# Mixture of experts: one rotating pool of tiles against fixed places with all weight loads on SyncE

## The chip, the cores and the metric

The kernel runs on one core of a Trainium2 chip. The metric is the device time of one execution in microseconds. TensorE is called PE, VectorE DVE, ScalarE ACT, GpSimd POOL and SyncE SP in the rows; PEld is PE's weight load. A "q" behind an engine's name (ACTq, SPq) marks its sequencer, which issues DMAs.

## The reference

One decoder layer on 1024 tokens of width 1024, all in float32. Three token mixers and a memory cross attention come first, each followed by a layer norm. The change lies in the last part, the routed experts: each token picks the best of 4 groups and the two best of the 8 experts in it, and the results of its two experts are added with their weights. The router is left out here:

```python
def one_expert(x_blk, ex):
    hidden = jax.nn.silu(x_blk @ w_gate[ex]) * (x_blk @ w_up[ex])   # 1024 -> 256
    return hidden @ w_down[ex]                                      # 256 -> 1024
# 32 experts; every token goes to 2 of them
y = jnp.einsum('nk,nkd->nd', expert_w, y_of_assignments)
x = layer_norm(alpha * x + y, ln3_g, ln3_b)
```

## The kernel before

The program is unrolled and runs in stages; the experts' stage (`moe`) follows the second layer norm with the router (`out_ln_route`) and is followed by the last layer norm (`final`). The normed rows stand in HBM twice: `x2d`, from which experts gather, and `acc`, to which experts add.

For each of the 32 experts up to 128 rows are gathered. Their steps, with the names that the planner gives them:

- `L`: the expert's weights come in six pieces of 128 x 1024 float32 (512 KB): four hold a quarter of gate and up (two DMAs of 256 KB), two hold half of down (one DMA). `moe_load` issues them.
- `SA`, `SD`: PE reads float32 in one quick pass only in a rounded format, so a piece is split into a rounded high part (ACT, line 1887) and the rest (DVE, line 1890), and three matmuls are made in place of one (lines 1645 to 1647). Experts 0 and 1 are not split but read whole (line 1643).
- `G`, `GQ`: the rows are gathered from `x2d` by an indirect DMA on POOL's queue (line 1616). `RT`, `RA`, `RD`: PE transposes them, ACT and DVE split them.
- `U` 0 to 3: the gate and up product with pieces 0 to 3. `YA`, `YD`: SiLU times up into a row tile `m_y`. `HT`, `HA`, `HD`: the hidden rows are transposed and split.
- `N` 0, 1: the down product with pieces 4 and 5. `EA`, `ED`: the result is scaled into the same `m_y`, half on ACT and half on DVE.
- `C`, `CQ`: an indirect DMA on POOL's queue adds `m_y` to `acc` (line 1706). The next scatter waits until this one has landed.

The order of all instructions on the five engines is fixed: `Plan.run` plays the tasks through with given lengths and lags and calls each task's function in the order of the start that it finds. Engine "Q" of the plan stands for the DMA engines.

Tiles of 4 KB a partition (`slot`) all come from one pool, `b4`, of 45 places. A tile gets a place when the function that needs it is called, and takes over the place of a tile that has been released; the first instruction that writes it waits for the last one that used the place. For an `m_y` that is the landing of its scatter. In the plan `SLOTS` (11) is the number of places that are to be had beside those of pieces already loaded and gathered rows; a load takes 1, a split 2, `YA` 1, and each gives back when done. 28 pieces are loaded by SP while the router still runs (`BEFORE`); the others are issued by ACT, in ACT's own order:

```python
def load(e, i):
    raw.setdefault(e, []).append(moe_load(k, ins, e, i, None, nc.scalar))

def split_hi(e, i):
    w[e, i] = [slot(k, "s" + n, (128, 2, HALF), F32R) for n in "hl"]
    nc.scalar.activation(w[e, i][0], raw[e][i], AF.Copy)
```

`overflow_blocks` is a loop for experts with more than 128 rows. The count is read at run time, and in the profiled execution its body doesn't run.

Of the kernel before, what the change touches and what calls it, by code (L numbers as in the profile page):

```python
# [8 lines left out]
F32 = mybir.dt.float32  # L9
# [1747 lines left out]
def overflow_blocks(k, ins, x2d, acc):  # L1757
    nc, tc = k.nc, k.tc
    n = nc.values_load(k.on[0:1, 0:1], min_val=0, max_val=15)
    with tc.If(n > 0), tc.For_i(0, n, 1) as i:  # L1760
        ids, firsts = overflow_list(k)
        e = nc.values_load(ids[0:1, bass.ds(i, 1)], engines=(E.SP,), min_val=0, max_val=NE - 1)
        raw, xg = slot(k, "m_raw", (128, 2, 2 * FF)), slot(k, "m_xg")
        parts = [slot(k, "m_w" + x, (128, 2, 2 * FF), F32R) for x in "hl"]

        first = k.sm.tile([128, 1], F32, tag="o_f", bufs=1)
        sel = k.sm.tile([128, 16], F32, tag="o_sel", bufs=1)
        nc.vector.tensor_scalar(sel, k.io128[:, 0:16], k.octr, None, op0=OP.is_equal)
        nc.vector.tensor_tensor(sel, sel, firsts, op=OP.mult)
        nc.vector.reduce_sum(first, sel, axis=AX.X)  # L1770
        nc.vector.tensor_scalar(k.octr, k.octr, 1.0, None, op0=OP.add)
        key = k.sm.tile([128, NT, 2], F32, tag="o_key", bufs=1)
        nc.vector.tensor_scalar(key, k.key, first, 1.0 / NE, op0=OP.subtract, op1=OP.mult)
        ps = k.ps.tile([128, 512], F32, tag="r")
        for t in range(NT):
            for j in range(2):
                nc.vector.tensor_scalar(k.R[j], k.io128, key[:, t, j:j + 1], None, op0=OP.is_equal)
                nc.tensor.matmul(ps[:, 0:2], k.R[j], k.ent[:, t, j], start=(t == 0 and j == 0),
                                 stop=(t == NT - 1 and j == 1))
        tab = k.sm.tile([128, 2, 1], F32, tag="o_tab", bufs=1)  # L1780
        slot_table(k, tab, ps[:, 0:2, None])
        nc.gpsimd.memset(xg, 0.0)
        moe_gather(k, tab, xg, x2d)

        def piece(j):
            return split_big(k, moe_load(k, ins, bass.ds(e, 1), j, raw), parts)

        for _ in moe_up(k, moe_rows(k, xg), piece, xg):
            pass
        _, h, _ = moe_hidden(k, xg)  # L1790
        _, pss = moe_down(k, h, lambda f: piece(4 + f))
        for n in range(2):
            moe_scale(k, pss, xg, tab, n)
        moe_scatter(k, xg, tab, acc)


class Plan:
# [4 lines left out]
    def __init__(self, slots, rest):  # L1802
        self.slots, self.rest, self.tasks, self.rank = slots, rest, {}, {}

    def add(self, name, engine, length, before=(), f=None, lag=0.15, take=0, give=0, release=0.0, rank=None):
        self.rank[name] = rank
        self.tasks[name] = engine, length, [b for b in before if (b[1] if b[0] == "then" else b) in self.tasks], f, lag, take, give, release

    def run(self):
        tail, after, need = {}, {n: [] for n in self.tasks}, {}  # L1810
        for n, (_, _, before, *_) in self.tasks.items():
            need[n] = len(before)
            for b in before:
                if b[0] == "then":
                    after[b[1]].append((n, 0))
                else:
                    after[b].append((n, 1))
        for n in reversed(self.tasks):
            tail[n] = self.tasks[n][1] + max((tail[m] + l * self.tasks[n][4] for m, l in after[n]), default=0.0)
            if self.rank[n] is not None:  # L1820
                tail[n] = self.rank[n]
        ready = {n: t[7] for n, t in self.tasks.items() if not need[n]}
        free, given, slots = {}, [], self.slots
        while ready:
            best = None
            for n, at in ready.items():
                e, _, _, _, _, take, _, _ = self.tasks[n]
                at = max(at, free.get(e, 0.0))
                if take:
                    have, rest = slots, self.rest if n[0] == "LS" else 0  # L1830
                    for g, m in given:
                        if have >= take + rest and g > at:
                            break
                        have += m
                        if have - m < take + rest:
                            at = max(at, g)
                    if have < take + rest:
                        continue
                first = ready[n] if e == "Q" else -tail[n]
                if best is None or (at, first) < best[:2]:  # L1840
                    best = at, first, n
# [4 lines left out]
            slots -= take  # L1846
            while given and given[0][0] <= at:
                slots += given.pop(0)[1]
            if give:
                given = sorted(given + [(at + length + lag, give)])  # L1850
# [9 lines left out]
def moe(k, ins, raw, x2d, acc):  # L1860

    nc = k.nc
    tab = [k.tabs[:, :, e:e + 1] for e in range(NE)]
    with k.tc.manual_schedule(engines=MOE_MANUAL):
# [9 lines left out]
    overflow_blocks(k, ins, x2d, acc)  # L1874

    P = Plan(SLOTS, REST)
    w, x, up, y, hid, h, down, pss = {}, {}, {}, {}, {}, {}, {}, {}

# [3 lines left out]
    def load(e, i):  # L1882
        raw.setdefault(e, []).append(moe_load(k, ins, e, i, None, nc.scalar))

    def split_hi(e, i):
        w[e, i] = [slot(k, "s" + n, (128, 2, HALF), F32R) for n in "hl"]
        nc.scalar.activation(w[e, i][0], raw[e][i], AF.Copy)  # L1887

    def split_lo(e, i):
        nc.vector.tensor_tensor(w[e, i][1], raw[e][i], w[e, i][0].bitcast(F32), op=OP.subtract)  # L1890

    def weights(e, i):
        return [raw[e][i]] if whole(e, i) else w.pop((e, i))
# [17 lines left out]
    def start_up(e):  # L1911
        up[e] = moe_up(k, x[e], lambda j: weights(e, j))
# [16 lines left out]
    order = [(e, i) for e in range(NE - LATE) for i in range(6)]  # L1929
    order += [(e, i) for p in (range(4), range(4, 6)) for e in range(NE - LATE, NE) for i in p]  # L1930
    for n, (e, i) in enumerate(order):
        if BEFORE[7][1] <= n < THEN:
            P.add(("L", e, i), "Q", 1.46, [], None, 0.9, release=FIRST)
        if n >= THEN:
            P.add(("LS", e, i), "A", 0.05, [("then", ("LS", *order[n - 1])), ("then", ("L", *order[n - AHEAD]))],
                  lambda e=e, i=i: load(e, i), 1.5, take=1, release=FIRST)
            P.add(("L", e, i), "Q", 1.46, [("LS", e, i)], None, 0.9)
    for e in range(NE):
        time = [1.72 if whole(e, i) else 1.3 for i in range(6)]
        for i in range(6):  # L1940
            if not whole(e, i):
                late = [] if e < SOON else [("U", e - 1, min(i, 3))]
                P.add(("SA", e, i), "A", 0.95, [("L", e, i)] + late, lambda e=e, i=i: split_hi(e, i), take=2)
                P.add(("SD", e, i), "D", 1.14, [("SA", e, i)], lambda e=e, i=i: split_lo(e, i), give=1)
        if e > 1:
            P.add(("G", e), "P", 1.04, [("RT", e - XG, 1)], lambda e=e: moe_gather(k, tab[e], k.xg[e % XG], x2d), 0.7,
                  release=4.0 * e if e < XG else 0.0)
            P.add(("GQ", e), "Q", 1.46, [("G", e)], None, 1.0)
        for g in range(2):
            P.add(("RT", e, g), "E", 0.44, [("GQ", e), ("RA", e - 1, g), ("RD", e - 1, g)],  # L1950
                  lambda e=e, g=g: rows(e, g), release=5.3 + 2.1 * e if e < 2 else 0.0)
            P.add(("RA", e, g), "A", 0.48, [("RT", e, g), ("U", e - 2, 3)], lambda e=e, g=g: rows_hi(e, g))
            if not whole(e, 0):
                P.add(("RD", e, g), "D", 0.6, [("RA", e, g)], lambda e=e, g=g: rows_lo(e, g))
        for j in range(4):
            before = [("L", e, j), ("SD", e, j), ("RA", e, j // 2), ("RD", e, j // 2), ("YD", e - 2), ("U", e, j - 1)]
            P.add(("U", e, j), "E", time[j], before, (lambda e=e: next(up[e])) if j else (lambda e=e: start_up(e)),
                  give=1 if whole(e, j) else 2)
        P.add(("YA", e), "A", 0.26, [("U", e, 3)], lambda e=e: silu(e), take=1)
        P.add(("YD", e), "D", 0.34, [("YA", e)], lambda e=e: next(up.pop(e)))  # L1960
        P.add(("HT", e), "E", 0.22, [("YD", e), ("HA", e - 1), ("HD", e - 1)], lambda e=e: start_hidden(e))
        P.add(("HA", e), "A", 0.26, [("HT", e), ("N", e - 1, 1)], lambda e=e: hidden_hi(e))
        if not whole(e, 4):
            P.add(("HD", e), "D", 0.34, [("HA", e)], lambda e=e: next(hid.pop(e)))
        for f in range(2):
            before = [("L", e, 4 + f), ("SD", e, 4 + f), ("HA", e), ("HD", e), ("EA", e - 1), ("ED", e - 1), ("N", e, f - 1)]
            P.add(("N", e, f), "E", time[4 + f], before, (lambda e=e: next(down.pop(e))) if f else (lambda e=e: start_down(e)),
                  give=1 if whole(e, 4 + f) else 2)
        P.add(("EA", e), "A", 0.57, [("N", e, 1)], lambda e=e: moe_scale(k, pss[e], y[e], tab[e], 0))
        P.add(("ED", e), "D", 0.66, [("N", e, 1)], lambda e=e: moe_scale(k, pss[e], y[e], tab[e], 1))  # L1970
        P.add(("C", e), "P", 1.04, [("EA", e), ("ED", e), ("CQ", e - 1)],
              lambda e=e: moe_scatter(k, y.pop(e), tab[e], acc), 0.7)
        P.add(("CQ", e), "Q", 1.46, [("C", e)], None, 1.0, give=1)
# [4 lines left out]
SLOTS, REST = 11, 1  # L1978
LATE = 2
WHOLE = (0, 1), (0, 1)  # L1980
AHEAD, FIRST, THEN = 3, 4.0, 28
XG = 4
SOON = 2
# [237 lines left out]
```

## Time and profile before

| | |
|---|---|
| time, median of 3 runs | 2030.04 us (2027.97 to 2032.48) |
| the profiled execution: time, span | 2029.34 us, 2027.6 us |
| before the experts / experts / last layer norm | 0 to 1617 / 1617 to 1991 / 1991 to 2028 us |
| PE, DVE, ACT busy over the span | 92%, 60%, 41% |
| DMA | 265.95 MB, mean 131 GB/s |

Times inside the profile are counted from the span's start. The profiled execution's time is 1.7 us more than its span: what lies before the first and behind the last instruction. A busy share over the whole span mixes stages with different limits, so the rows below are taken from the experts' stage alone.

### The profile page before, as it was taken

The numbers are of one execution on the slowest core, as the hardware profiler recorded it, in microseconds if no ns is written. First come the engines' busy times: TensorE is split into PE (matmuls) and PEld (weight loads), VectorE is DVE, ScalarE is ACT, GpSimd is POOL, SyncE is SP. The second block draws the span as 40 slices with busy tenths as digits, with TensorE's granted clock in tenths as the row PEclk, the third lists the DMA queues.
The fourth block names the chain that finished last, engine by engine and source line by source line (L and its number), as shares of the span: only waits on it lengthen the run. The fifth ranks groups of instructions, "written<-read, shape, count | busy, mean of one in ns | idle before, by whom it ended". The sixth has DMA issues, their size and how long they took to land. (4 is left out here: it accounts for less than half of the span.)

```text
span 2027.6 us, 26514 instructions
## 1 busy us (share of the span) xinstructions
PE 1874.6 (92%) x9820; PEld 1521.3 (75%) x9820; DVE 1213.4 (60%) x2629; ACT 840.3 (41%) x1454; POOL 224.1 (11%) x261
## 2 busy tenths in 40 slices
PE   7999999999999999999989999899989689998890
PEld 6777787787877788888877788888877557876670
DVE  3244376676766543424455767544577648997885
ACT  3433232333332353535443312433421148876773
POOL 2000000000000010000003100000001222332310
PEclk8999999999999999999999999999999899999995
DMA  4113123232314122122525323710345577999995
GB/s 129 33 32 84 42 83 79 63 99 63 99 53 105 57 63 73 53 84 68 167 84 200 119 101 108 197 28 25 115 166 179 188 254 248 294 308 313 303 302 187
DMA packets 201653, 265.95 MB, mean 131 GB/s; under 512 B 24490, under 2 KB 132200, under 8 KB 201520
## 3 DMA queue, kind: packets, MB, share of 16 engines
q1 hardware_dynamic: 148992, 149.45, 23.6%
q10 hardware_dynamic: 39264, 86.07, 12.3%
q0 software_dynamic: 13264, 28.71, 6.0%
q8 instruction: 78, 1.28, 0.3%
q14 instruction: 55, 0.45, 0.1%
HBM read 228.95 MB, written 51.97 MB: 139 GB/s over the span
## 5 line engine op out<-in xcount | busy, mean ns | idle before, releaser
L142 PE MATMUL ps<-thh,hi 128*128 128x512 f32 x1152 | 467.7, 406 | 5.2 <-ACT hi L52 1.9
L143 PE MATMUL ps<-thl,hi 128*128 128x512 f32 x1152 | 456.4, 396 | 0.0
L144 PE MATMUL ps<-thh,lo 128*128 128x512 f32 x1152 | 455.7, 396 | 0.0
L142 PEld LDWEIGHTS ps<-thh,hi 128*128 128x128 f32 x1152 | 218.0, 189 | 51.5 <-issue 6.0
L144 PEld LDWEIGHTS ps<-thh,lo 128*128 128x128 f32 x1152 | 217.5, 189 | 45.8 <-issue 1.1
L143 PEld LDWEIGHTS ps<-thl,hi 128*128 128x128 f32 x1152 | 218.2, 189 | 38.8 <-issue 0.3
L1890 DVE TENSOR_TENSOR sl<-m_raw,sh 128x1024 fp32r<-128x1024 f32 x180 | 214.2, 1219 | 41.2 <-ACT sh L1887 31.6
L1887 ACT ACTIVATE sh<-m_raw 128x1024 fp32r<-128x1024 f32 x180 | 186.1, 1059 | 36.4 <-DMA acc<-m_y,r_big 13.0
L53 DVE TENSOR_TENSOR lo<-raw,hi 128x1024 fp32r<-128x1024 f32 x64 | 78.3, 1224 | 117.1 <-ACT hi L52 105.9
L52 ACT ACTIVATE hi<-raw 128x1024 fp32r<-128x1024 f32 x64 | 67.8, 1059 | 139.8 <-PE ps L143 120.1
L1646 PE MATMUL ps<-sl,m_xhi 128*128 128x512 f32 x240 | 97.6, 407 | 15.2 <-DVE sl L1890 14.5
L1645 PE MATMUL ps<-sh,m_xhi 128*128 128x512 f32 x240 | 101.1, 421 | 2.7 <-ACT sh L1887 2.7
L1647 PE MATMUL ps<-sh,m_xlo 128*128 128x512 f32 x240 | 95.9, 400 | 1.5 <-DVE m_xlo L1909 1.5
L783 DVE CUSTOM_DVE_ANT_0 f_P<-S,f_c 128x1024 f32<-128x1024 f32 (+7 forms) x64 | 48.4, 757 | 80.9 <-PE S L780 78.5
L1706 POOL DMA_INDIRECT acc<-m_y,r_big x32 | 60.3, 1883 | 205.8 <-ACT sh L1887 51.0
L1053 PE MATMUL ps<-ohi,hi 128*128 128x512 f32 x192 | 77.1, 402 | 1.5 <-DVE mt L1061 1.5
L791 ACT ACTIVATE f_P<-f_P,nm 128x1024 f32<-128x1024 f32 (+7 forms) x64 | 49.8, 778 | 65.7 <-DVE nm L783 65.4
L1055 PE MATMUL ps<-ohi,lo 128*128 128x512 f32 x192 | 75.5, 393 | 0.0
L1054 PE MATMUL ps<-olo,hi 128*128 128x512 f32 x192 | 75.3, 392 | 0.0
L1646 PEld LDWEIGHTS ps<-sl,m_xhi 128*128 128x128 f32 x240 | 45.9, 191 | 30.9 <-DVE sl L1890 22.4
L718 POOL TENSOR_SCALAR_AFFINE_SELECT f_c<-f_c 128x128 f32<-128x128 f32 x64 | 22.5, 351 | 388.8 <-DVE nm L783 363.6
L801 ACT COPY f_PT<-ps 128x512 f32<-128x512 f32 (+3 forms) x96 | 43.4, 479 | 46.1 <-PE ps L800 37.3
(489 smaller groups left out, 3733.2 us busy)
## 6 DMA issues: line engine op xcount, KB each, us to landing
raw<-in_w_in SPq DMA_DIRECT2D x64, 512.0 KB, 4.2
m_raw<-in_moe_w_down ACTq DMA_DIRECT2D x56, 512.0 KB, 5.9
m_raw<-in_moe_w_gate ACTq DMA_DIRECT2D x108, 256.0 KB, 5.9
m_raw<-in_moe_w_up ACTq DMA_DIRECT2D x108, 256.0 KB, 6.3
gate<-gt SPq DMA_DIRECT2D x24, 512.0 KB, 3.0
mt<-gate SPq DMA_DIRECT2D x24, 512.0 KB, 5.3
wraw<-in_xa_wkv SPq DMA_DIRECT2D x16, 512.0 KB, 7.5
m_raw<-in_moe_w_gate SPq DMA_DIRECT2D x20, 256.0 KB, 4.8
```

The lines of the kernel that those rows point to most:

```text
L53: k.nc.vector.tensor_tensor(lo, src, hi.bitcast(F32), op=OP.subtract)
L142: k.nc.tensor.matmul(ps[:, :n], hi[:, d], xh, start=(d == 0), stop=False)
L143: k.nc.tensor.matmul(ps[:, :n], hi[:, d], xl, start=False, stop=False)
L144: k.nc.tensor.matmul(ps[:, :n], lo[:, d], xh, start=False, stop=(d == ND - 1))
L1053: nc.tensor.matmul(ps, whi[:, f], hi[:, s], start=(f == 0), stop=False)
L1054: nc.tensor.matmul(ps, whi[:, f], lo[:, s], start=False, stop=False)
L1055: nc.tensor.matmul(ps, wlo[:, f], hi[:, s], start=False, stop=(f == 3))
L1645: nc.tensor.matmul(ps, x[0], w[0], start=start, stop=False)
L1646: nc.tensor.matmul(ps, x[0], w[1], start=False, stop=False)
L1647: nc.tensor.matmul(ps, x[1], w[0], start=False, stop=stop)
L1887: nc.scalar.activation(w[e, i][0], raw[e][i], AF.Copy)
L1890: nc.vector.tensor_tensor(w[e, i][1], raw[e][i], w[e, i][0].bitcast(F32), op=OP.subtract)
```

## The change

The pool's places are given out by hand, once, ahead of the experts:

- 29 places for raw pieces (`RAWS`). Piece number n of the order of loads uses place n modulo 29. A load waits for the last reader of the piece that was there: the second half of its split, or the product if it is read whole.
- 4 pairs for split pieces (`PAIRS`), handed from the product that is done with one to the next split. 3 places for `m_y` (`YS`): `YA` of an expert waits for the scatter three experts before. 3 for gathered rows (`XG`, 4 before).
- All loads of the stage are issued by SP, in the order of the pieces (`then` the load before). One more is issued ahead of the loop, number 28.
- The condition that a split waits for a product of the expert before (`SOON`) goes, as do `SLOTS`, `REST` and `AHEAD`. The plan's lengths and lags are changed for nearly all tasks (a first half of a split 1.06 instead of 0.95, a load 1.6 instead of 1.46, a gather's or scatter's lag 4.0 instead of 1.0), and its tails are computed in an order that follows the tasks' conditions.
- `overflow_blocks` uses one of the fixed pairs and two of the `m_y` places.

The core of the diff (the planner's bookkeeping of places and the other changed lengths are left out):

```diff
-        for j in range(BEFORE[7][1], THEN):
+        for j in range(len(rawt), RAWS):
             t = slot(k, "m_raw", (128, 2, 2 * FF))
             nc.gpsimd.memset(t[0:1, 0, 0:1], 0.0)
-            raw.setdefault(j // 6, []).append(moe_load(k, ins, j // 6, j % 6, t))
+            rawt.append(moe_load(k, ins, *order[j], t))
         for i in range(2, XG):
             k.xg.append(slot(k, "m_xg"))
             nc.vector.memset(k.xg[i], 0.0)
...
+    ys = [slot(k, "m_y", (128, 2, HALF)) for i in range(YS)]
+    pairs = [[slot(k, "s" + n, (128, 2, HALF), F32R) for n in "hl"] for i in range(PAIRS)]
...
-    def load(e, i):
-        raw.setdefault(e, []).append(moe_load(k, ins, e, i, None, nc.scalar))
+    def tile(e, i):
+        return rawt[at[e, i] % RAWS]
 
     def split_hi(e, i):
-        w[e, i] = [slot(k, "s" + n, (128, 2, HALF), F32R) for n in "hl"]
-        nc.scalar.activation(w[e, i][0], raw[e][i], AF.Copy)
+        w[e, i] = pairs.pop(0)
+        nc.scalar.activation(w[e, i][0], tile(e, i), AF.Copy)
...
     def weights(e, i):
-        return [raw[e][i]] if whole(e, i) else w.pop((e, i))
+        if whole(e, i):
+            return [tile(e, i)]
+        pairs.append(w[e, i])
+        return w.pop((e, i))
...
-        if n >= THEN:
-            P.add(("LS", e, i), "A", 0.05, [("then", ("LS", *order[n - 1])), ("then", ("L", *order[n - AHEAD]))],
-                  lambda e=e, i=i: load(e, i), 1.5, take=1, release=FIRST)
-            P.add(("L", e, i), "Q", 1.46, [("LS", e, i)], None, 0.9)
+        last = order[n - RAWS] if n >= RAWS else None
+        before = [] if last is None else [("U" if last[1] < 4 else "N", last[0], last[1] % 4) if whole(*last) else ("SD", *last)]
+        P.add(("L", e, i), "Q", LOAD, [], None if n < RAWS else lambda e=e, i=i: moe_load(k, ins, e, i, tile(e, i)), 1.5,
+              release=FIRST if n >= THERE else -100.0)
+        if n:
+            before.append(("then", ("L", *order[n - 1])))
...
-        P.add(("YA", e), "A", 0.26, [("U", e, 3)], lambda e=e: silu(e), take=1)
+        P.add(("YA", e), "A", 0.4, [("U", e, 3), ("CQ", e - YS)], lambda e=e: silu(e))
...
-SLOTS, REST = 11, 1
-AHEAD, FIRST, THEN = 3, 4.0, 28
-XG = 4
-SOON = 2
+FIRST, THERE, LOAD = 4.0, 28, 1.6
+XG, YS, PAIRS, RAWS = 3, 3, 4, 29
```

## Rows read from the trace of the kernel before

**Rows 1.** Windows: busy us of PE, PEld, DVE, ACT, POOL; clock, DMA, GB/s.

```profile
1617.00:1648.00 31.00, 24.70 (x70) 13.10 (x69) 7.27 (x14) 11.93 (x16) 6.15 (x6) 0.79 0.74 247
1648.00:1740.00 92.00, 82.42 (x382) 66.20 (x381) 75.04 (x88) 66.85 (x92) 27.37 (x17) 0.98 0.80 248
1740.00:1783.00 43.00, 42.25 (x207) 35.35 (x205) 41.44 (x50) 35.91 (x49) 17.79 (x10) 1.00 0.94 308
1783.00:1848.00 65.00, 58.15 (x274) 46.41 (x273) 56.11 (x66) 45.12 (x62) 20.64 (x13) 1.00 0.96 310
1848.00:1940.00 92.00, 79.31 (x350) 62.15 (x348) 73.76 (x85) 64.20 (x86) 22.31 (x14) 0.96 0.93 307
1940.00:1975.00 35.00, 34.18 (x157) 27.42 (x158) 32.48 (x39) 26.66 (x36) 7.10 (x5) 1.00 0.93 308
```

**Rows 2.** Windows, the stretch in which DVE is fullest.

```profile
1730.00:1805.00 75.00, 74.07 (x366) 62.11 (x365) 72.48 (x87) 60.05 (x83) 29.81 (x16) 1.00 0.94 303
```

**Rows 3.** Chain that ended last, in order of time: start, us, what.

```profile
1650.37 9.61 DMA acc<-m_y,r_big
...
1894.76 9.31 DMA m_raw<-in_moe_w_up
```

**Rows 4.** Line 1887, 1645 to 1775: ACT idle until (us, times).

```profile
  DMA acc<-m_y,r_big: 13.0, 6
```

**Rows 5.** The same, 1775 to 1975.

```profile
  DMA m_raw<-in_moe_w_up: 9.4, 19
...
  issue: 1.4, 5
```

**Rows 6.** Groups by line, 1630 to 1985: count, busy us, mean ns, idle.

```profile
L1890 DVE TENSOR_TENSOR sl<-m_raw,sh 128x1024 fp32r<-128x1024 f32 x180 | 214.2, 1219 | 41.2 <-ACT sh L1887 31.6 <-DMA acc<-m_y,r_big 8.8
L1887 ACT ACTIVATE sh<-m_raw 128x1024 fp32r<-128x1024 f32 x180 | 186.1, 1059 | 36.4 <-DMA acc<-m_y,r_big 13.0 <-DMA m_raw<-in_moe_w_up 9.4 <-DMA m_raw<-in_moe_w_down 5.9
```

**Rows 7.** Timeline of SP: first load of the last stage.

```profile
1990.71 4.14 SPq L2015 DMA_DIRECT2D f_row<-acc  x8
```

**Rows 8.** DMA, 1617 to 1975: bytes in all, and the GpSimd queue's.

```profile
DMA packets 48121, 102.78 MB, mean 287 GB/s; under 512 B 9264, under 2 KB 9264, under 8 KB 48095
...
q0 software_dynamic: 8927, 16.47, 18.8%
```

**Rows 9.** Line 1643, 1617 to 1660: matmuls on whole pieces.

```profile
L1643 PE MATMUL ps<-m_raw,m_xhi x32: 592/592/1220, 1625.3 to 1644.5; 128*128 128x512 f32 x32
...
L1643 PE MATMUL ps<-m_raw,m_hr x16: 590/592/592, 1641.5 to 1657.8; 128*128 128x512 f32 x16
```

**Rows 10.** Timeline of ACT: the last split.

```profile
1975.06 1.06 ACT L1887 ACTIVATE sh<-m_raw 128x1024 fp32r<-128x1024 f32 x1 [1.54 <-DMA m_raw<-in_moe_w_down]
```

**Rows 11.** Line 1887 (first half of a split): how many (x).

```profile
1620.00:1785.00 165.00, 83.81 (x83) 0.96 0.84 268
1620.00:1805.00 185.00, 92.93 (x91) 0.96 0.85 272
```

**Rows 12.** Line 1647 (third matmul, two a piece): how many (x).

```profile
1640.00:1785.00 145.00, 60.32 (x152) 29.16 (x153) 0.99 0.84 265
1640.00:1805.00 165.00, 69.80 (x176) 33.48 (x176) 0.99 0.85 270
```

**Rows 13.** Line 1706 (scatter), 1740 to 1848: ns, first and last start, landing.

```profile
L1706 POOL DMA_INDIRECT acc<-m_y,r_big x11: 1592/1787/2332, 1740.8 to 1837.7; - x11
...
DMA to landing us min/median/max: 7.5/9.0/9.8
```

**Rows 14.** Line 1706, 1648 to 1740: issue to landing.

```profile
DMA to landing us min/median/max: 6.5/8.4/9.6
```

**Rows 15.** Line 1616 (gather), 1648 to 1912: issue to landing.

```profile
DMA to landing us min/median/max: 4.2/8.5/10.0
```

**Rows 16.** Timeline of DVE ahead of the experts.

```profile
1611.98 0.91 DVE L1873 MEMSET m_xg<- 128x1024 f32 x1 [0.16 <-issue]
1612.82 0.16 DVE L1398 TENSOR_TENSOR A<-r_iou,j 128x64 bf16<-128x64 uint32 x1
```

More of the change, by code (lines that the diff above doesn't have):

```diff
@@ L1754, in overflow_list, with overflow_blocks @@
     return ids, first
-def overflow_blocks(k, ins, x2d, acc):
+def overflow_blocks(k, ins, x2d, acc, raw, xg, parts):
     nc, tc = k.nc, k.tc
@@ L1797, with __init__, add @@
 class Plan:
[L1802 to L1807, printed above, removed]
+    def __init__(self, pairs):
+        self.pairs, self.tasks = pairs, {}
+    def add(self, name, engine, length, before=(), f=None, lag=0.15, take=0, give=0, release=0.0):
+        self.tasks[name] = engine, length, [b for b in before if b in self.tasks], f, lag, take, give, release
     def run(self):
-        tail, after, need = {}, {n: [] for n in self.tasks}, {}
+        after, need = {n: [] for n in self.tasks}, {}
         for n, (_, _, before, *_) in self.tasks.items():
@@ L1813, in run @@
             for b in before:
[L1814 to L1818, printed above, removed]
+                then = b[0] == "then"
+                after[b[1] if then else b].append((n, 0.0 if then else 1.0))
+        line, left = [n for n in self.tasks if not need[n]], dict(need)
+        for n in line:
+            for m, _ in after[n]:
+                left[m] -= 1
+                if not left[m]:
+                    line.append(m)
+        tail = {}
+        for n in reversed(line):
             tail[n] = self.tasks[n][1] + max((tail[m] + l * self.tasks[n][4] for m, l in after[n]), default=0.0)
-            if self.rank[n] is not None:
-                tail[n] = self.rank[n]
         ready = {n: t[7] for n, t in self.tasks.items() if not need[n]}
-        free, given, slots = {}, [], self.slots
+        free, given, pairs = {}, [], self.pairs
         while ready:
@@ L1828, in run @@
                 at = max(at, free.get(e, 0.0))
[L1829 to L1837, printed above, removed]
+                if take and not pairs:
+                    if not given:
                         continue
+                    at = max(at, given[0])
                 first = ready[n] if e == "Q" else -tail[n]
@@ L1845, in run @@
             free[e] = at + length
-            slots -= take
-            while given and given[0][0] <= at:
-                slots += given.pop(0)[1]
+            while given and given[0] <= at:
+                pairs += 1
+                given.pop(0)
+            pairs -= take
             if give:
-                given = sorted(given + [(at + length + lag, give)])
+                given = sorted(given + [at + length + lag])
             for m, l in after[n]:
@@ L1863, in moe @@
     tab = [k.tabs[:, :, e:e + 1] for e in range(NE)]
+    order = [(e, i) for e in range(NE - LATE) for i in range(6)]
+    order += [(e, i) for p in (range(4), range(4, 6)) for e in range(NE - LATE, NE) for i in p]
+    rawt = [t for e in sorted(raw) for t in raw[e]]
     with k.tc.manual_schedule(engines=MOE_MANUAL):
@@ L1911, in start_up @@
     def start_up(e):
-        up[e] = moe_up(k, x[e], lambda j: weights(e, j))
+        up[e] = moe_up(k, x[e], lambda j: weights(e, j), yv[e % YS])
         next(up[e])
@@ L1927, in start_down @@
         pss[e] = next(down[e])
[L1929 to L1930 removed]
     for n, (e, i) in enumerate(order):
[L1932 to L1937 removed]
+        last = order[n - RAWS] if n >= RAWS else None
[4 more added lines that the diff above has]
+            before.append(("then", ("L", *order[n - 1])))
+        P.tasks["L", e, i][2].extend(before)
     for e in range(NE):
[L1939 removed]
+        time = [1.72 if whole(e, i) else 1.37 for i in range(6)]
         for i in range(6):
             if not whole(e, i):
[L1942 to L1944 removed]
+                P.add(("SA", e, i), "A", 1.06, [("L", e, i)], lambda e=e, i=i: split_hi(e, i), take=1)
+                P.add(("SD", e, i), "D", 1.22, [("SA", e, i)], lambda e=e, i=i: split_lo(e, i))
         if e > 1:
[L1946 removed]
+            P.add(("G", e), "P", 1.04, [("RT", e - XG, 1)], lambda e=e: moe_gather(k, tab[e], k.xg[e % XG], x2d), 1.0,
                   release=4.0 * e if e < XG else 0.0)
[L1948 removed]
+            P.add(("GQ", e), "Q", 1.1, [("G", e)], None, 4.0)
         for g in range(2):
```

32 lines of the change are left out of this document (16 added, 16 removed).

## The prediction, made before the changed kernel ran

> **What bounds the kernel now.** I read the page's busy time by slices first. PE is 92% busy over the whole span, but the diff touches only the experts, from about 1617 us to the last scatter, so the first view that counts is the windows of that stage [rows 1]. Look at the two last columns. From 1648 to 1740 the DMA engines are 80% busy and move 248 GB/s, DVE works 75.0 of 92 us and PE 82.4: nothing is full. From 1740 on the DMA engines are 93 to 96% busy at 307 to 310 GB/s, 308 as their mean, and that is how it stays until the last weight load. The first 123 us are slack; the last 235 are a DMA-bound stage.
>
> The chain of waits says what the slack waits for [rows 3]: early it runs through the landing of a scatter (9.61 us), late through the landing of a gate or up load (9.31 us). The waits of line 1887, the first half of a split, draw the border. Up to 1775 a split stood 13.0 us, in six waits, for a scatter and for no load [rows 4]; after that it waits for loads, 9.4 us in 19 short waits for `moe_w_up` alone [rows 5]. In the code a split's tile, a load's tile and an outgoing row all come out of one pool of 45 places. A place last used by `m_y` is free only once its scatter has landed, and the next tile that gets it waits. When that tile is a split or a load on ACT's queue, all that stands behind it on ACT waits too, DVE's half of the split first (8.8 us of its idle time directly for scatters, 31.6 for the first half [rows 6]). Loads that could have run early run late, the store of loaded pieces empties, and from about 1775 every split meets a load that has just landed.
>
> **The change, part by part.** I take the changes against the profiled execution: 2029.34 us, 0.7 under the median 2030.04 of the three runs; the stage ends with the first reload of `acc` at 1990.71 [rows 7], and the 37 us after it are not touched.
>
> *Loads on SyncE into 29 fixed places.* A load now waits for one thing, the last reader of the piece 29 before it, and nothing but loads queues behind it until the last stage. So the 248 GB/s stretch should run at the 308 of the later one. The stage moved 102.78 MB up to 1975 [rows 8]; 164 pieces of 0.524 MB are 86.0 of that, and the GpSimd queue's 16.47 MB over its 32 gathers, 30 scatters and one parameter load make 0.26 MB each. The start gets worse, though. Before, the spare places let loads start at once (74% busy up to 1648). Now piece 28 goes out early, and 29 to 32 each wait for a whole piece that PE reads in the up product, 1625.3 to 1644.5 [rows 9]. Pieces 33 and 34 take the places of expert 0's down pieces, whose first reading is at 1641.5 [rows 9]; SyncE's queue is in order, so 35 to 38, whose places are free sooner, stand behind them. I count eleven pieces and five gathers by 1650, 5.8 and 1.3 MB. The other 95.7 MB at 308 GB/s take 311 us, so the last piece lands at 1961. Bounds: no stop at all, 101.6 MB from the first of these reads on, 1626, ends at 1956. If the pieces behind expert 1's down product also wait until its last reading at 1657.8 [rows 9], some 94.7 MB are left there, and the end is 1965. If the rate grows to a full 100% (308/0.94 = 328 GB/s), it is 1942. I take 1961 because the 308 was measured with the same gathers and scatters beside it.
>
> After the last load the old kernel needs 15.65 us: its last split waits for its load until 1975.06 [rows 10], the reload goes out at 1990.71 [rows 7]. With the same tail the stage ends at 1976.7, a gain of 14.0 us.
>
> *Loads off ACT.* The issues of the 164 pieces leave ACT's queue. Their own time is hidden under ACT's work: line 1887 lost 1.4 us to issues after 1775 [rows 5]. I count nothing more for it than what the places bring; the upper end is those 1.4 us. A page of the Trainium skill ("DMA: Bandwidth & Descriptors", section "Issuing engines are not separate DMA queues") says that transfers from all issuing engines run on the same 16 DMA engines, so that another issuer saves only issue time; by it this part alone is worth at most those 1.4 us, and the little idle time in the row agrees.
>
> *Four fixed pairs for split pieces.* Before, ACT could run far ahead. At 1785 line 1887 had run 83 times [rows 11] and the third matmul, two for each piece, 152 times [rows 12]: seven pairs live. At 1805 it was 91 against 88: three. In those 20 us PE used twelve pieces, 1.67 us each. With a mean of five live, a pair lived 8.3 us; with three at the same pace 5.0. Four pairs at 8.3 us give 2.08 us a piece, at 5.0 they give 1.25; the work itself (1.06 and 1.22 us for the halves [rows 6], six matmuls of 0.2 us, by the 366 in 74.1 us of [rows 2]) bounds it below at 0.87. The long lives hold queueing that a limit removes, so I take the middle of the two, 6.7 us and 1.67 a piece. From 1648 the 176 pieces beyond the first four (of 180) then end at 1942, ahead of the loads: cost nothing, covered by the loads. Where no pair is free, a first half waits on ACT, behind it SiLU and the scaling of rows, and DVE and PE behind those; 2.08 a piece, without any cover, would end them at 2014 on the span's clock, 39 us later than now.
>
> *Engines.* DVE has 278.8 us of work from 1648 to 1975 (sum of [rows 1]); at the 72.48 of 75 us that it reached [rows 2] this takes 289 us, to 1937. PE's 1370 matmuls at 0.202 us take 277. Both stay behind the loads.
>
> *Three places for outgoing rows.* The scatters are a chain of their own: each waits for the landing of the one before, since both add into `acc`. From 1740 to 1848 eleven ran back to back, 1740.8 to 1837.7, so 9.69 us a cycle with a median landing of 9.0 [rows 13]. At 80% busy DMA the landing was 8.4 [rows 14], so full DMA would add 0.2. First scatter at 1650.4 [rows 3], 32 cycles of 9.9: it ends at 1967, ten under 1976.7. The third place lets SiLU of an expert wait for the scatter three before it, two cycles of slack, so nothing is added; if it did wait, first halves of splits would stand behind it on ACT.
>
> *Three gathered rows instead of four.* A gather goes out when its row tile has been read and is needed three experts later, about 30 us; a scatter ahead of it on GpSimd's queue can hold it 9.7, and it lands in 8.5, at most 10.0 [rows 15]. Hidden. Without the cover it would be the overrun, up to a few us an expert.
>
> *One clearing less.* DVE clears two more gathered-row tiles just ahead of the experts; the second (0.91 us) stands directly before the routing's last mask at 1612.82 [rows 16]. It goes: between 0 and 0.9 us; I take 0.9, as the next operation starts with its end. Sum: 2029.3 - 14.0 - 0.9 = 2014.
>
> **The rivals.** (a) *The pairs throttle.* The loop pair free, ACT, DVE, PE, pair free limits everything. It ends later than now once a piece takes over (1975 - 1648)/176 = 1.86 us, so from a pair's life of 7.4 us. At 7.9, midway to the 8.3 seen, 1.98 us a piece end at 1996: 21 us late, about 2049. For it: ACT had seven pairs out in the fastest stretch. Against: three carried the same pace at 1805. (b) *The scatters become the chain.* If fuller DMA engines brought every landing to the longest seen, 9.8, a cycle is 10.5 and the chain ends at 1986: 2024. It would be slower than now only from a cycle of 10.6. (c) *The loads go full speed.* 328 GB/s end them at 1942; then the scatters end the stage at 1967, a gain of 24: 2005. Against: 96% is the most that a window of [rows 1] shows. (d) *It does nothing.* The early 248 GB/s were not for want of places but of work on PE and DVE; then loads come earlier, are used at the same pace, and only issue and clearing time (1.4 + 0.9) go: 2027. Against: the waits of [rows 4], which the change takes away. The Trainium skill's section named above, read as all that the change is, would end here.
>
> **How the numbers follow.** The forecast, loads continuous at about 308 GB/s, has 0.58, with its own range from 2008 (no stop at the start, 5 us, and a little more rate) to 2024 (10 us lost to stops of the loads, DVE and the scatters, each of which is over 90% full up to 1961). (c) has 0.10, (b) 0.08, (d) 0.10, (a) 0.14. About 0.2%, 4 us, is what a measurement of this kernel can tell from no change, which puts (d) and a quarter of (b) in the middle: faster 0.74, same 0.12, slower 0.14. The range must leave out (a) and the far part of (c): 2004 to 2031.
>
> **What would show it.** Right: no wait of a split for a scatter; about 308 GB/s in every window from 1650 on; the last load landing near 1961; splits that wait for no load until late in the stage; SyncE stopped at expert 0's and 1's down pieces near 1640. Wrong: windows from 1650 on at 250 to 280 GB/s with ACT's first halves waiting for PE (then the pairs), scatters back to back with landings over 10 us, or DVE and PE idle for rows that GpSimd's queue holds up. If the rate is 308 from 1650 and the gain still fails to come, the sum of bytes or the tail was wrong.

## The result, and the profile after

The changed kernel takes 2016.55 us (median of 4 runs, 2014.75 to 2019.60), the kernel before 2030.28 in the same session: a ratio of 0.9934, interval 0.9917 to 0.9951. Run again in a later session it took 2021.66 (12 runs) against 2030.58, 0.9958 (0.9937 to 0.9979). The forecast was 2014 in a range of 2004 to 2031. The sign and the size hold; a good part of the way there does not, as the experiments show.

The profiled execution took 2019.60 us. In the new file the first half of a split is line 1890, the second 1893, the row transposes 1907. The windows of the stage, as in [rows 1]:

```profile
1617.00:1648.00 31.00, 28.46 (x83) 14.31 (x82) 8.20 (x11) 13.28 (x19) 6.41 (x5) 0.92 0.62 201
1648.00:1740.00 92.00, 84.67 (x386) 65.90 (x385) 78.25 (x89) 66.97 (x89) 25.76 (x19) 0.98 0.96 322
1740.00:1783.00 43.00, 39.49 (x182) 30.61 (x181) 38.54 (x44) 32.59 (x44) 11.13 (x8) 1.00 0.96 330
1783.00:1848.00 65.00, 59.22 (x276) 46.93 (x275) 57.75 (x67) 49.98 (x66) 18.97 (x13) 1.00 0.99 321
1848.00:1940.00 92.00, 84.26 (x389) 66.42 (x388) 81.38 (x92) 70.88 (x94) 25.59 (x16) 1.00 0.94 311
1940.00:1975.00 35.00, 30.93 (x135) 23.65 (x135) 28.86 (x35) 24.05 (x32) 7.93 (x4) 1.00 0.40 105
```

The loads do what was forecast: 311 to 330 GB/s from 1648 on instead of 248 at first, and 105 in the last window, where they are through. But look at the counts of PE. From 1648 to 1740 the DMA engines move 30% more than before and PE runs 386 matmuls instead of 382. The weights lie there earlier and are used no faster. (The changed kernel's stage begins 6.4 us earlier, so its windows stand 6.4 us later in the stage than those of [rows 1].) ACT's waits, 1645 to 1965 (us in total, times, longest), say for what a first half of a split stands:

```profile
ACT sh L1890 <- PE ps L1647: 58.3, 97, 2.6
ACT sh L1890 <- DVE sl L1893: 8.9, 7, 1.3
...
ACT sh L1890 <- DMA m_raw<-in_moe_w_up: 0.3, 1, 0.3
```

The waits for scatters of [rows 4] are gone and those for loads of [rows 5] nearly so; 58 us of waiting for the third matmul on a piece, that is for a free pair, stand in their place. The end of the stage, in the timeline of SP (start, us), is the last issue of loads and then the first reload:

```profile
1939.74 2.60 SPq L1610 DMA_DIRECT2D m_raw<-in_moe_w_down  x4
1981.76 3.77 SPq L2018 DMA_DIRECT2D f_row<-acc  x8
```

The last load lands at 1952.2, and the reload comes 29.6 us later. Before, 15.65 us lay between.

Where the stage gained and where it lost shows in the scalings of rows on ACT, one for each of the 32 experts. The 16th and the 32nd, in the kernel before and then in the changed one (start, us):

```profile
1804.65 0.67 ACT L1700 ACTIVATE m_y<-ps,r_big 128x512 f32<-128x512 f32 x1
1980.06 0.69 ACT L1700 ACTIVATE m_y<-ps,r_big 128x512 f32<-128x512 f32 x1 [3.09 <-PE ps L1647]
```

```profile
1808.88 0.69 ACT L1700 ACTIVATE m_y<-ps,r_big 128x512 f32<-128x512 f32 x1
1973.40 0.69 ACT L1700 ACTIVATE m_y<-ps,r_big 128x512 f32<-128x512 f32 x1 [2.44 <-PE ps L1647]
```

Counted from the first gather, the 16th comes at 187.0 us before and at 197.7 now, and the next sixteen take 175.4 before and 164.5 now. The second execution of each kernel gives the same (189.0 and 175.6; 197.7 and 164.5). So the half of the stage that was bound by loads became 11 us shorter, and the first half 9 to 11 us longer.

From the first gather to the first reload, the stage took 373.1 us before (1617.63 to [rows 7]) and 370.5 now (1611.23 to 1981.76). Of the 9.7 us between the two profiled executions the stage is 2.6. Another 0.8 come after the reload (36.9 to 36.1). Ahead of the stage, GpSimd's wait for the routing shrinks by 1.8, as both clearings of [rows 16] left DVE's path: one is gone, the other now runs behind the routing's last step. The remaining 4.5 lie in code that is the same. No profile shows them to be the change's: in the seven of kernels with the old early code the first gather starts at 1610.7 to 1619.7 us, in the seven with the changed one at 1608.4 to 1619.5, and the two means lie 1.4 us apart, no more than the clearings.

### The profile page after: what moved, and what is told of

Its sections match the earlier page's. It is cut to its first block, busy times and chain, and to the rows that moved or that the text cites. A ratio compares the mean times of both kernels' runs of the same rounds, so it can differ in the third digit from the quotient of the medians.

```text
span 2017.9 us, 26760 instructions
## 1 busy us (share of the span) xinstructions
PE 1874.5 (93%) x9820; PEld 1515.3 (75%) x9820; DVE 1217.4 (60%) x2628; ACT 844.4 (42%) x1454; POOL 218.2 (11%) x262
## 5 line engine op out<-in xcount | busy, mean ns | idle before, releaser
L1893 DVE TENSOR_TENSOR sl<-m_raw,sh 128x1024 fp32r<-128x1024 f32 x180 | 219.4, 1223 | 37.0 <-ACT sh L1890 30.2
L1890 ACT ACTIVATE sh<-m_raw 128x1024 fp32r<-128x1024 f32 x180 | 190.9, 1061 | 68.8 <-PE ps L1647 58.9
```

The source lines that it names most:

```text
L1890: nc.scalar.activation(w[e, i][0], tile(e, i), AF.Copy)
L1893: nc.vector.tensor_tensor(w[e, i][1], tile(e, i), w[e, i][0].bitcast(F32), op=OP.subtract)
```

## The experiments

All stage times are from the first gather to the first reload in the profiled execution. The three groups of runs were made on three chips; beside them the kernel before had 2030.58, 2030.64 and 2030.83 us. Times of different groups are best compared by their ratios.

| kernel | time, us | ratio to before | stage, us |
|---|---|---|---|
| before, profiled twice | 2030.6 | 1 | 373.1, 375.4 |
| changed (and again) | 2016.55 (2021.66) | 0.9934 (0.9958) | 370.5 (370.7) |
| 3 pairs | 2045.37 | 1.0067 [1.0048, 1.0087] | 395.3 |
| 6 pairs, 25 raw | 2020.68 | 0.9940 [0.9919, 0.9960] | 369.4 |
| 5 pairs, 28 raw, 2 rows | 2031.81 | 1.0010 [0.9989, 1.0030] | 380.7 |
| 4 pairs, 21 raw | 2025.79 | 0.9970 [0.9951, 0.9988] | 373.8 |
| changed, loads on ACT | 2110.41 | 1.0392 [1.0366, 1.0418] | 457.8 |
| before, loads on SP | 2026.57 | 0.9975 [0.9952, 0.9999] | 376.5 |
| before, fixed rows | 2008.12 | 0.9891 [0.9866, 0.9917] | 356.2 |
| the same, XG 3 | 2012.45 | 0.9909 [0.9875, 0.9944] | 358.7 |
| before, fixed rows, loads on SP | 2002.35 | 0.9867 [0.9832, 0.9902] | 350.8 |
| the same, 4 fixed pairs | 2008.95 | 0.9902 [0.9866, 0.9939] | 352.8 |

**Is it the pairs?** Four runs change the numbers of places alone. First the changed kernel as it is:

> The changed kernel once more, to see what of its 13.7 us lies in the experts' stage and what ahead of it. In the first pair of profiles the experts' first gather went out 6.4 us earlier (1611.2 against 1617.6) and the stage itself, from there to the reload of acc, was only some 2 us shorter (about 371 against 373 us). If the stage is what was gained, a second profile shows it at 360 to 365 us; if the earlier part differed by chance (TensorE at its lower clock in other places), the stage is again near 371 and the time again near 2016.

It came back with the same stage, 370.7 us, while its time was 5 us higher. Then one pair fewer, two more (paid for by four raw places), and eight raw places fewer:

```diff
-XG, YS, PAIRS, RAWS = 3, 3, 4, 29
+XG, YS, PAIRS, RAWS = 3, 3, 3, 29     # 3 pairs
+XG, YS, PAIRS, RAWS = 3, 3, 6, 25     # 6 pairs
+XG, YS, PAIRS, RAWS = 3, 3, 4, 21     # 21 raw
```

> Three pairs instead of four, all else as in the changed kernel. P: between 5.5 and 7.4 us of life over three pairs, 1.85 to 2.45 us a piece instead of 1.8, so 20 to 110 us slower: 2035 to 2125. L and E: 2013 to 2020, since loads and order of the engines stay.

> Six pairs for split pieces instead of four, 25 places for raw pieces instead of 29 (25 loaded ahead). Theory P (the pairs limit: four live all the time, a pair's life 7.4 us): with six at the same life 1.25 us a piece would do, so VectorE becomes the limit at 9.6 to 9.9 us an expert instead of 10.4 to 11.2, 12 to 20 us less than the changed kernel: 1997 to 2005. Theory L (the loads limit, as predicted blind): no gain, and four places fewer may cost some: 2015 to 2022. Theory E (the order of the engines' work limits, whatever the pairs): 2013 to 2019.

> 21 places for raw pieces instead of 29, 21 loaded ahead; four pairs. In the changed kernel's profile a piece has landed 47 us (early) to 16 us (late) ahead of its split. P and E: eight places are some 14 us of that lead, so it stays above zero and the time is 2013 to 2020. L: the loads start later and the end moves with them, by up to eight pieces of 1.7 us: 2025 to 2031.

Three pairs cost 24 us, so the pairs do bind. Six take the waiting for a pair away, 2.5 us instead of 58.3 (first line, 1645 to 1965), and win one microsecond, which the intervals do not tell from none. At the 16th scaling this kernel is 6.6 us ahead of the changed one (191.1 against 197.7), but it takes 2.7 more for the next sixteen. ACT now waits for products and, from 1885 on, splits wait for loads again (second line), as the 25 raw places are used up:

```profile
ACT sh L1890 <- PE ps L1647: 2.5, 4, 0.9
ACT sh L1890 <- DMA m_raw<-in_moe_w_up: 6.5, 6, 2.4
```

With 21 raw places the time is 4 us longer, as theory L had it (2025 to 2031), though splits wait 1.4 us for loads in the whole stage. So no mix of these sizes moves the stage much below 370 us. One more mix took its two places from outgoing rows and raw pieces:

> The changed kernel with one more pair for split pieces (5 instead of 4), paid for by one place for outgoing rows (2 instead of 3) and one for raw pieces (28 instead of 29). From the runs so far 3 pairs cost 24 us, 6 pairs gained about 9 us in the middle of the stage and lost it at the end through 4 raw places fewer. Theory P (pairs and raw pieces share a budget, and the changed kernel stands a pair short): faster than the changed kernel by 2 to 7 us, 2010 to 2015, ACT waits well under the 58.9 us for a free pair, and no split waits for a load for over 2 us in all. Theory E (the order written by the planner and PE at 91 to 92% hold it): within 3 us of it, 2015 to 2021. If SiLU then waits for scatters two experts back, it is slower, 2022 or more, and ACT shows waits for the landing of acc.

It is the third case of that text: with two places SiLU waits for scatters, and the splits behind it on ACT with it.

```profile
ACT m_y L1663 <- DMA acc<-m_y,r_big: 32.0, 16, 4.4
```

**The parts one by one.** The loads' queue alone, on the old pool and on the fixed places, is one word in each kernel (`nc.scalar` to `nc.sync` and back):

> The kernel before with one word changed: its weight loads are issued by SyncE instead of ACT; the rotating pool of 45 places stays. Theory Q (the queue matters: a load that waits for a place stopped ACT and the splits behind it): most of the gain of the change shows, 2016 to 2021 us, and first halves of splits lose well under the 13.0 us that they lost to scatters up to 1775. Theory S (it is the order in which places come free that matters: a split that gets a place last held by an outgoing row waits itself, whoever issues the loads): 2027 to 2032, with the 13 us still there, and issue time of 1 to 2 us saved at most.

> The changed kernel with one word changed: its weight loads go out on ACT's queue instead of SyncE's; the fixed places stay. Theory Q: each load that waits for the last reader of its place now stops ACT, and with it the splits; the gain is lost, 2027 us or more, and ACT shows waits for PE or DVE at the load's lines. Theory S: the fixed places carry the gain and the planner puts each load on ACT after its reader is done, so the time is within 4 us of the changed kernel, 2013 to 2024, with the issues' own 1 to 3 us the only loss.

On the old pool the queue gives 4 us (the interval just leaves out none), and the stage of its profile is no shorter. That is close to theory S's time; of its sign, the 13.0 us that splits stood for scatters, one wait of 6.7 is left. SP now stands for scatters in ACT's stead:

```profile
SPq L1607 <- DMA acc<-m_y,r_big: 53.1, 7, 11.7
```

On the fixed places the queue is worth 89 us (2110.41 against 2021.66). That is theory Q's time, but its sign, ACT waiting for PE or DVE at the loads' lines, is missing: no load on ACT shows a wait of its own. From 1660 on, 111 of 163 loads go out within 0.06 us of the start of the split ahead of them, here one that had stood for a pair:

```profile
1699.71 1.06 ACT L1890 ACTIVATE sh<-m_raw 128x1024 fp32r<-128x1024 f32 x1 [2.21 <-PE ps L1647]
1699.71 0.33 ACTq L1607 DMA_DIRECT2D m_raw<-in_moe_w_gate  x1
```

So a load stands there behind splits that wait, and what comes late makes later splits wait: from 1648 to 1740 the DMA engines move 221 GB/s instead of 322, and the splits wait 71 us for loads. Next the outgoing rows alone, loads on ACT, everything else rotating:

```diff
+    ys = [slot(k, "m_y", (128, 2, HALF)).rearrange("p a b -> p (a b)") for i in range(YS)]
...
-        P.add(("YA", e), "A", 0.26, [("U", e, 3)], lambda e=e: silu(e), take=1)
+        P.add(("YA", e), "A", 0.26, [("U", e, 3), ("CQ", e - YS)], lambda e=e: silu(e))
...
-SLOTS, REST = 11, 1
+SLOTS, REST, YS = 8, 1, 3
```

> The kernel before with one part of the change alone: outgoing rows have three fixed places, taken in turn, and the pool that split pieces and loads rotate through is planned with 8 free places instead of 11. Loads stay on ACT. Theory S (scatters' places in the pool were the loss): no split waits for a scatter, and the time falls by 5 to 13 us, to 2017 to 2025. Theory P (what counts is how far splits and loads may run ahead in all, and the three places are missed elsewhere): 2027 to 2034, with the scatter's waits replaced by waits for PE or for loads.

2008.12 us, eight less than the whole change in its first session and 13.5 less than in its second. No split waits for a scatter any more, and the 16th scaling comes 172.7 us after the first gather instead of 187.0. The edit also plans with 8 free places instead of 11, which was not tried alone. Its window against the second line of [rows 1]: PE at 91.66 of 92 us and 440 matmuls, with 301 GB/s.

```profile
1648.00:1740.00 92.00, 91.66 (x440) 75.61 (x439) 87.88 (x104) 79.96 (x108) 37.88 (x19) 1.00 0.92 301
```

**The parts put together.** On the fixed rows, each further part of the change was added, and the kernel before was profiled once more:

> The kernel before with two parts of the change: the three fixed places for outgoing rows, and the loads issued by SyncE. Split pieces and raw pieces still rotate through one pool. The rows alone gave 2008 us, the loads on SyncE alone 2027. Theory A (rows' places are the whole gain; the shared pool for splits and raw pieces is better than fixed pairs and fixed raw places): 2003 to 2011, at least 5 us below the changed kernel. Theory Q (a load that waits on SyncE's queue in order does the harm in the changed kernel): 2013 or more, with splits waiting for loads.

> The kernel before with the three fixed places for outgoing rows and, from the change too, three gathered rows instead of four; the place that comes free goes to the pool (planned with 9 free places). Theory A (places in the shared pool are what counts, gathers are hidden): 2003 to 2008, splits waiting for loads under the 28 us that they lost with eight. Theory G (the fourth gathered row was needed): over 2010, with transposes waiting for the landing of gathered rows.

> The kernel before with the fixed places for outgoing rows, the loads on SyncE, and four fixed pairs for split pieces; raw pieces alone rotate through what is left of the pool (28 places and none spare). What is left of the change are the fixed raw places, three gathered rows instead of four and the durations that the planner works with. Theory P (the fixed pairs are what gives the rows' gain back): 2016 to 2024, ACT waiting over 40 us for PE's last reader of a pair. Theory E (planner or raw places in turn): within 4 us of the kernel with rows and SyncE alone.

> The kernel before, unchanged, for a second profile. The first had 373.1 us from the first gather to the first reload of acc, and 1617.6 us ahead of it. If these are typical, both come back within 2 us. If the first profile had a favourable stage and an unfavourable start, the stage takes 376 to 380 us and the start about 1613, as in the kernels that share its early code.

Rows and SP together are the fastest kernel of this study, 2002.35 us, 14 to 19 below the changed one. The queue's share shows in the splits' waits for loads, first with the loads on ACT, then on SP (1645 to 1965, both):

```profile
ACT sh L1888 <- DMA m_raw<-in_moe_w_up: 14.8, 16, 3.3
ACT sh L1888 <- DMA m_raw<-in_moe_w_down: 13.6, 17, 2.9
```

```profile
ACT sh L1888 <- DMA m_raw<-in_moe_w_up: 5.5, 9, 1.1
ACT sh L1888 <- DMA m_raw<-in_moe_w_down: 0.4, 2, 0.2
```

A gathered row fewer, with its place given to the pool, made it 4 us slower by the medians (intervals overlap), not faster. Theory A's sign came, 10.2 us of waits for loads instead of 28.4, without its time; theory G's time came without its sign. So with loads on ACT these waits say little about the time. The second profile of the kernel before had the first expectation's start (1619.7) and between the two in its stage, 375.4.

Four fixed pairs on top of rows and SP are the run that decides. The edit takes the splits' tiles from a list, as the change does, and keeps the old planner, the old lengths, four gathered rows and a rotating pool of 28 for raw pieces:

```diff
-        w[e, i] = [slot(k, "s" + n, (128, 2, HALF), F32R) for n in "hl"]
+        w[e, i] = pairs.pop(0)
...
-        return [raw[e][i]] if whole(e, i) else w.pop((e, i))
+        if whole(e, i):
+            return [raw[e][i]]
+        pairs.append(w[e, i])
+        return w.pop((e, i))
...
-SLOTS, REST, YS = 8, 1, 3
+SLOTS, REST, YS, PAIRS = 0, 0, 3, 4
```

The splits wait 41 us for a pair, as theory P said, and it costs next to nothing: 352.8 us of stage instead of 350.8, 6.6 us by medians whose intervals overlap. Its time lies below theory P's range and just above theory E's.

```profile
ACT sh L1901 <- PE ps L1647: 41.2, 83, 2.0
```

So four pairs by themselves do not hold a kernel at 370. The difference lies in the first half: four pairs in the old planner's order reach the 16th scaling 169.9 us after the first gather, six in the changed planner's only at 191.1. What these two kernels do differently with four pairs each stands in ACT's timeline (start, us, line, idle before). First one expert of the kernel with rows, SP and four pairs, from one scaling of rows (line 1700) to the next:

```profile
1710.62 0.67 ACT L1700 ACTIVATE m_y<-ps,r_big 128x512 f32<-128x512 f32 x1
1711.18 1.05 ACT L1901 ACTIVATE sh<-m_raw 128x1024 fp32r<-128x1024 f32 x1
...
1713.10 1.06 ACT L1901 ACTIVATE sh<-m_raw 128x1024 fp32r<-128x1024 f32 x1
1714.07 0.58 ACT L1922 ACTIVATE m_xhi<-ps 128x512 fp32r<-128x512 f32 x1
1715.06 1.07 ACT L1901 ACTIVATE sh<-m_raw 128x1024 fp32r<-128x1024 f32 x1 [0.41 <-PE ps L1647]
1716.02 0.36 ACT L1663 ACTIVATE m_y<-ps 128x256 f32<-128x256 f32 x1
1716.41 1.06 ACT L1901 ACTIVATE sh<-m_raw 128x1024 fp32r<-128x1024 f32 x1
1717.78 1.06 ACT L1901 ACTIVATE sh<-m_raw 128x1024 fp32r<-128x1024 f32 x1 [0.30 <-PE ps L1647]
1719.13 1.06 ACT L1901 ACTIVATE sh<-m_raw 128x1024 fp32r<-128x1024 f32 x1 [0.30 <-PE ps L1647]
1720.10 0.67 ACT L1700 ACTIVATE m_y<-ps,r_big 128x512 f32<-128x512 f32 x1
```

And the changed kernel:

```profile
1709.45 0.36 ACT L1663 ACTIVATE m_y<-ps 128x256 f32<-128x256 f32 x1
1709.71 0.68 ACT L1700 ACTIVATE m_y<-ps,r_big 128x512 f32<-128x512 f32 x1
1710.28 0.59 ACT L1911 ACTIVATE m_xhi<-ps 128x512 fp32r<-128x512 f32 x1
1710.76 1.06 ACT L1890 ACTIVATE sh<-m_raw 128x1024 fp32r<-128x1024 f32 x1
...
1712.32 1.06 ACT L1890 ACTIVATE sh<-m_raw 128x1024 fp32r<-128x1024 f32 x1
1713.29 0.37 ACT L1678 ACTIVATE m_hr<-pt 128x256 fp32r<-128x256 f32 x1
1715.05 1.06 ACT L1890 ACTIVATE sh<-m_raw 128x1024 fp32r<-128x1024 f32 x1 [1.40 <-PE ps L1647]
1716.90 1.06 ACT L1890 ACTIVATE sh<-m_raw 128x1024 fp32r<-128x1024 f32 x1 [0.79 <-PE ps L1647]
1718.28 1.06 ACT L1890 ACTIVATE sh<-m_raw 128x1024 fp32r<-128x1024 f32 x1 [0.32 <-PE ps L1647]
1719.64 1.06 ACT L1890 ACTIVATE sh<-m_raw 128x1024 fp32r<-128x1024 f32 x1 [0.29 <-PE ps L1647]
1720.61 0.36 ACT L1663 ACTIVATE m_y<-ps 128x256 f32<-128x256 f32 x1
1720.87 0.68 ACT L1700 ACTIVATE m_y<-ps,r_big 128x512 f32<-128x512 f32 x1
```

Six splits stand in both, but one expert takes 9.48 us (1710.62 to 1720.10) in the first and 11.16 (1709.71 to 1720.87) in the second. In the first, SiLU, the scaling and the first halves of rows (line 1922) lie apart from one another, and the splits shown wait at most 0.41 us for a pair. In the second SiLU, scaling and first halves of rows come in one bunch, 1709.45 to 1710.76, and the two splits behind it don't wait: pairs were free and ACT came late. After them four splits in a row wait for pairs, 2.80 us in all. PE pays directly behind the bunch:

```profile
1710.86 0.50 PE L1646 MATMUL ps<-sl,m_xhi 128*128 128x512 f32 x1 [0.76 <-DVE sl L1893]
```

From 1645 to 1800 PE's waits for DVE's half of a split come to this, first with the old order and then in the changed kernel (us, times, longest):

```profile
PE ps L1646 <- DVE sl L1904: 0.9, 2, 0.6
```

```profile
PE ps L1646 <- DVE sl L1893: 9.5, 12, 1.3
```

That order is written out by the planner ahead of time. The period of the changed kernel is 11.14 to 11.17 us for seven experts in a row, and 11.15 or 11.16 in its second execution; before, the same experts took 8.8 to 12.3. Two executions that repeat to a few hundredths speak for a fixed order and against contention.

PE's order differs in the same way. With U for an up piece, N for a down piece, r for four row transposes and H for the transposes of the hidden rows, the kernel before and those with fixed rows and loads on ACT, loads on SP and four pairs write H U r U N U N U r for most of the early experts, the changed kernel H r U r U N U N U. SiLU and its multiplication stand between an expert's last U and its H: in the first order PE has four products and the row transposes in that time, in the second two. For the experts of the steady stretch, DVE's multiplication ends 3.1 us before H in the kernel with rows, SP and four pairs and 0.3 us before it in the changed one.

## Why the prediction was right, and where it was not

**Loads: right, on their own clock.** Predicted: a stop of SP near 1640, 308 GB/s from 1650 on, the last landing at 1961. SP waited 23.9 us in ten waits for line 1643 (14.0 at line 1610, 9.9 at line 1607), the longest of them, 8.3, for expert 0's first up piece; the last load that had waited for a down piece there went out at 1638.1, 1644.5 on the clock of before. The rate was 311 to 330, so rival (c)'s rate partly came too. The last landing, 1952.2, is 1958.6 on the clock of before (6.4 us later at the first gather). What this was to bring came too: the sixteen experts of the second half took 10.9 us less.

**The tail: the step that failed.** "With the same tail the stage ends at 1976.7" took over the 15.65 us from a kernel whose splits waited for loads. Now no split waits for one, and the tail was 29.6 us. The gain of 14.0 for the stage measured 2.6 (4.7 in the second pair of profiles). The term behind it is the pace that the four pairs were given, 1.67 us a piece, so that they would "cost nothing, covered by the loads". In the steady stretch it was 11.16/6 = 1.86, the break-even of rival (a); from the first scaling of rows to the last, 336.1 us for 31 experts, it was 1.81. It shows in the first half of the stage, where 9 to 11 us were lost. But its reason is not the number of pairs alone. In the old order four pairs run a piece in 9.48/6 = 1.58 in the first half and in 1.67 from the first scaling to the last (311.0 us), the assumed pace, so (a) as written falls as well.

**What was left out.** The diff changes the planner's lengths, lags, tails and conditions, and the forecast gave the order that results no term at all. From the kernel with rows, SP and four pairs (352.8) to the changed one (370.5) the stage is 17.7 us longer: 27.7 up to the 16th scaling, less 10 after it, where the changed kernel has loads in store. Between them lie this order, raw pieces taken in turn, and three gathered rows for four. The last cost 2.5 us of stage where it was tried (358.7 against 356.2). The fixed raw places let loads land tens of microseconds ahead of their splits early on, and splits wait 0.3 us for gate and up loads in all. That leaves the order, and the two timelines show it at work. It is the likeliest cause and not a shown one: it was not undone by itself, nor is it settled which of the planner's edits (lengths, the dropped condition, tails that run on through the loads) writes it.

**Outgoing rows: right, and worth more than the sum.** The reading of [rows 3] and [rows 4], that places held until a scatter lands hold up splits and loads, is borne out by the run with fixed rows alone: 16.9 us less of stage, 22 of time. The forecast gave these three places nothing of their own ("so nothing is added") and booked the gain on the loads and all fixed places together.

**The loads' issuer: too small.** Counted as nothing, at most 1.4 us. (Those 1.4 us were misread: "issue" in [rows 5] is idle time of ACT for which the profile shows no releaser, not the time of issuing loads.) On the rotating pool it gave 4 us, on fixed rows 5.4 of stage and 6 of time (overlapping intervals), and fixed places without it lose 89. What the 89 are is not issue time. On fixed places a load that stands on ACT goes out when ACT comes to it, behind splits that wait. The Trainium skill ("DMA: Bandwidth & Descriptors", section "Issuing engines are not separate DMA queues") counts the sequencer's issue time as the only saving; the 89 us of one changed word show another, the place of a load in the issuing engine's order. On the rotating pool the gains are small, and by which mechanism is not shown.

**Scatters, gathers, clearing.** No split waited for a scatter, and landings from 1740 to 1848 stayed at 8.9 us (9.0 in [rows 13]), so rival (b) did not come. The clearings gave 1.8 instead of 0.9, since the planner's preamble let the second one fall behind the routing too. Rival (d) has its point: the early part was not used faster in this kernel, but slower.

So the total came out near the forecast in good part by luck. The profiled pair gained 9.7 us, of which the stage, the clearings and the end are 5.2; 4.5 are the chance of where the stage begins. The other three runs of the first session, 2014.75 to 2017.30 us, have no trace, and twelve more runs gained 8.9.

## What to carry to other kernels

When tiles of different life share one rotating pool, look for the longest life first: three places taken out for the rows that wait for a scatter were worth more than the whole of the larger change. Look at a stage in halves, too: here a gain in one hid a loss in the other. When a change touches a planner, give the order it will write a term of its own, compare the order of instructions on each engine, and cost an extra bunch of small operations where a scarce buffer comes free. A tail measured behind one limit may not be carried over to a kernel that the limit has left.

## What had not been expected of the hardware

Single runs of one kernel differ by 10 to 20 us, and the mean granted clock of TensorE in the run tells which. Of the 63 runs of the kernel before beside the experiments, 26 had a mean clock of 0.965 to 0.970 (up to 2043.0 us); the others (three chips together), grouped by that clock, stand beside the 12 of the changed kernel run again:

| mean granted clock | 0.971 | 0.972 | 0.973 | 0.974 | 0.975 | 0.976 | 0.977 |
|---|---|---|---|---|---|---|---|
| before, mean us (runs) | 2031.7 (12) | 2028.9 (10) | 2027.7 (8) | 2026.3 (6) | 2023.0 (1) | none | none |
| changed again, mean us (runs) | 2031.4 (1) | 2028.7 (1) | 2027.5 (1) | 2027.1 (1) | 2022.5 (1) | 2021.0 (4) | 2019.8 (3) |
| fixed rows, loads on ACT, mean us (runs) | none | 2013.3 (1) | none | 2008.0 (1) | 2007.7 (2) | none | none |

At an equal clock the changed kernel is no faster than before (five of its runs); the kernel with fixed rows is, by 15 to 18 us. That does not say that the change brings nothing. The mean clock is taken over the whole run, the stage included, and there the change raised it: from the first gather to the first reload it is 0.96 and 0.95 in the two profiles before, and 0.97 in both of the changed kernel. So at an equal mean clock a changed run will as a rule have had a lower clock elsewhere. The rise lies late in the stage (1.00 against 0.96 from 1848 to 1940), where the splits of the kernel before waited for loads [rows 5]. The first window, 0.92 against 0.79, shows none: counted from the first gather, the clock of the first 31 us is 0.80 before and 0.82 now, and the difference comes from the 6.4 us by which the stage began earlier.
